# Dealing the rows of a contraction to partitions in fours, and loading one operand by halves of its rows, in a two-layer matmul with GELU

## The chip, the cores and the metric

One core of one Trainium2 chip. The metric is device time in microseconds, the median of several executions. The kernel before takes 124.92 us (three runs, 124.63 to 124.98). Profiles are of one execution each, and their spans are 1.7 to 2.0 us shorter than the device time. In the views PE is TensorE, PEld its weight loads, DVE VectorE, ACT ScalarE and POOL GpSimd.

## The reference

```python
# a 1024x1024, b 1024x2048, c 2048x1024, all float32
h = a @ b
h = 0.5*h*(1 + tanh(sqrt(2/pi)*(h + 0.044715*h**3)))
return h @ c
```

## The kernel before

The first product is made with its rows h transposed: b is the stationary operand, a turned by 90 degrees (`aT`) the moving one. The second is one level of a Strassen scheme over 2x2 blocks. The change concerns the first stage: the first 512 rows of a against the first 768 columns of b, in eight slices of k of 128 each.

```python
av = a.rearrange("(mt p) k -> p mt k", p=128)
bv = b.rearrange("(kt p) n -> p kt n", p=128)      # slice k: 128 rows in succession
# ...
for k, n in ((0, 1), (1, 1), (2, 2), (4, 2), (6, 2)):
    load_a0(k, n)            # n*128 columns of 512 rows: runs of 512 or 1024 bytes
    for i in range(n):
        load_b0(k + i)       # 768 columns of 128 rows: runs of 3 KB
nc.gpsimd.tensor_copy(gate, b_st[5][:, 0:1])       # GpSimd's own loads start when b_5 has landed
# ... ten matmuls on zeros, to warm TensorE up ...
for k in range(KT):
    ab = abf.tile([128, 4, 128], BF16, name="ab")
    nc.vector.tensor_copy(ab, a_st[k])             # cast
    pt = tpool.tile([128, H], BF16, name="pt")
    for j in range(4):
        nc.tensor.transpose(pt[:, ts(j, 128)], ab[:, j, :], ident)
    nc.vector.tensor_copy(aT[0][:, k, :], pt)      # copy out of PSUM
    for i in range(2):
        nc.scalar.activation(b_lo[:, k, ts(i, W0 // 2)], b_st[k][:, ts(i, W0 // 2)], AF.Copy)
    if k > 0:
        mm0(k - 1)                                 # six matmuls 128x512 of the slice before
mm0(KT - 1)
# ... next columns of b (loaded by GpSimd), the other half of a, and so on: PE without a break ...
```

## Time and profile before

| | before |
|---|---|
| median | 124.92 us |
| span of the profiled run | 123.0 us |
| first matmul of the first stage | 7.87 us |
| first matmul of the stage after it | 22.10 us |

The last two are read from the timeline (start, length, engine, line, operation):

```profile
7.87 1.46 PE L102 MATMUL ps<-aT,b_lo 128*128 128x512 bf16 x6
...
22.10 0.60 PE L134 MATMUL pt<-aT,b_lo 128*128 128x512 bf16 x2
```

The page of the profile has a row per engine over the span in 40 equal slices (about 3.1 us each). A digit is the busy share in tenths; PEclk is the granted clock of TensorE; GB/s is what the DMA engines moved. Of the kernel before:

```profile
PE   6955889999998999999999999999999999999990
...
PEclk9999999999999999999999999999999999999997
...
GB/s 108 198 358 384 379 295 193 205 202 203 212 206 206 316 398 238 206 208 103 0 3 0 5 0 0 0 0 55 201 0 0 5 85 113 143 195 146 171 143 113
```

After the seventh slice PE is nearly full to the end, and in this run the clock is granted to the last slice. What can move the time is in the first six slices, where PE waits.

### The profile page before, as it was taken

The page shows a single profiled execution, that of the slowest core. Times are in us where ns is not written, and L with a number is a line of the kernel's source. Part 1 is how long each engine was busy: PE and PEld are TensorE (multiplying, and loading weights), DVE is VectorE, ACT ScalarE, POOL GpSimd, SP SyncE. Part 2 cuts the span into 40 slices and gives each one's busy share as a digit, 9 for nine tenths or more (in the row PEclk, how much of TensorE's full clock was granted, in tenths as well). Part 3 has the DMA queues.
Part 4 walks back from the last instruction along what each step waited for, and adds up shares of the span by engine and source line. Part 5 has one row for each costly group of instructions (what it writes and reads, how often), then busy time and mean ns, then how long its engine had stood idle before and what let it go on. Part 6 is the DMA issues. An engine that isn't in the chain of part 4 may idle for free.

```text
span 123.0 us, 1436 instructions
## 1 busy us (share of the span) xinstructions
PE 114.0 (93%) x555; PEld 66.8 (54%) x562; DVE 65.2 (53%) x94; ACT 29.6 (24%) x54; POOL 21.1 (17%) x26
## 2 busy tenths in 40 slices
PE   6955889999998999999999999999999999999990
PEld 2323444444456444444444444468888888888860
DVE  0233533000015200007999999999669999964440
ACT  4034545806331133233323333000000000000000
POOL 2000099133440210000000000995000000000000
PEclk9999999999999999999999999999999999999997
DMA  3899999999999999996000000001500023353433
GB/s 108 198 358 384 379 295 193 205 202 203 212 206 206 316 398 238 206 208 103 0 3 0 5 0 0 0 0 55 201 0 0 5 85 113 143 195 146 171 143 113
DMA packets 14213, 18.43 MB, mean 150 GB/s; under 512 B 768, under 2 KB 9728, under 8 KB 14208
## 3 DMA queue, kind: packets, MB, share of 16 engines
q0 software_dynamic: 7968, 8.91, 39.4%
q1 hardware_dynamic: 6240, 9.44, 22.0%
q8 instruction: 4, 0.07, 0.2%
q14 instruction: 1, 0.01, 0.0%
HBM read 20.97 MB, written 4.19 MB: 205 GB/s over the span
## 4 chain that ended last, share of the span: by engine, by line
PE 82%; DMA 12%; DVE 1%; SPq 1%; issue 1%; DVEq 0%
PE ps L246 41%; PE ps L143 31%; DMA a_st<-in_a_dram 12%; PE ps L102 3%; PE ps L134 3%; PE pt L134 3%; PE pt L162 1%; DVE aT L163 1%; PE pt L110 1%; DVE ab L107 0%; SPq L82 0%; SPq L76 0%; DVE ot L316 0%; DVEq L107 0%
## 5 line engine op out<-in xcount | busy, mean ns | idle before, releaser
L119 ACT ACTIVATE h<-ps 128x512 fp32r<-128x512 f32 (+1 forms) x30 | 17.3, 602 | 27.5 <-PE ps L143 25.2
L143 PE MATMUL ps<-aT,b_hi 128*128 128x512 bf16 x93 | 21.2, 379 | 0.2
L143 PE MATMUL ps<-aT,b_lo 128*128 128x512 bf16 x79 | 17.4, 379 | 0.1
L143 PEld LDWEIGHTS <-b_hi 128*128 128x128 bf16 x96 | 9.3, 98 | 10.8
L246 PE MATMUL ps<-t,s 128*128 128x512 f32 x64 | 15.1, 393 | 0.0
L246 PE MATMUL ps<-t,h 128*128 128x512 f32 x64 | 14.8, 389 | 0.0
L246 PE MATMUL ps<-c,h 128*128 128x512 bf16 (+1 forms) x71 | 14.1, 355 | 0.1
L246 PEld LDWEIGHTS ps<-t,s 128*128 128x128 f32 x64 | 12.0, 188 | 2.6
L246 PEld LDWEIGHTS ps<-t,h 128*128 128x128 f32 x64 | 12.0, 188 | 2.5
L286 POOL COPY lk<-u 128x512 f32<-128x512 f32 x1 | 7.6, 7579 | 33.5 <-ACT u L279 33.5
L143 PEld LDWEIGHTS <-b_lo 128*128 128x128 bf16 x80 | 7.8, 98 | 9.4
L200 DVE TENSOR_TENSOR t<-c,c 128x1024 fp32r<-128x1024 bf16 x4 | 4.7, 1222 | 15.4 <-DMA c<-in_c_dram 15.1
L163 DVE COPY aT<-pt 128x1024 bf16<-128x1024 bf16 x4 | 2.7, 688 | 18.1 <-PE pt L162 18.0
L102 PE MATMUL ps<-aT,b_lo 128*128 128x512 bf16 x47 | 11.5, 379 | 0.1
L246 PEld LDWEIGHTS <-h 128*128 128x128 bf16 x72 | 7.0, 98 | 7.0 <-issue 0.3
L113 ACT ACTIVATE b_lo<-b_st 128x384 bf16<-128x384 f32 x16 | 7.5, 515 | 10.2 <-DMA b_st<-in_b_dram 10.0
L188 POOL DMA_DIRECT2D c<-in_c_dram x8 | 5.9, 743 | 12.3 <-PE ps L143 6.0
L269 DVE TENSOR_TENSOR ot<-ps,u 128x512 f32<-128x512 f32 x11 | 7.3, 682 | 1.1 <-PE ps L246 1.1
L246 PE MATMUL ps<-c,s 128*128 128x512 f32 x32 | 7.4, 389 | 0.0
L107 DVE CAST ab<-a_st 128x512 bf16<-128x512 f32 x8 | 3.7, 463 | 6.0 <-DMA a_st<-in_a_dram 6.0
L246 PEld LDWEIGHTS ps<-c,s 128*128 128x128 f32 x32 | 6.0, 188 | 1.2
L110 PE MATMUL pt<-ident,ab 128*128 128x128 bf16 x32 | 3.2, 223 | 3.7 <-DVE ab L107 3.7
(37 smaller groups left out, 91.4 us busy)
## 6 DMA issues: line engine op xcount, KB each, us to landing
out_dram<-ot SPq DMA_DIRECT2D x15, 256.0 KB, 2.0
b_st<-in_b_dram SPq DMA_DIRECT2D x8, 384.0 KB, 8.6
c<-in_c_dram POOLq DMA_DIRECT2D x6, 512.0 KB, 14.7
c<-in_c_dram POOLq DMA_DIRECT2D x2, 1024.0 KB, 15.0
a_st<-in_a_dram SPq DMA_DIRECT2D x3, 512.0 KB, 8.9
b_hi<-in_b_dram POOLq DMA_DIRECT2D x4, 384.0 KB, 11.2
b_lo<-in_b_dram POOLq DMA_DIRECT2D x2, 512.0 KB, 7.1
ab<-in_a_dram POOLq DMA_DIRECT2D x4, 256.0 KB, 13.8
```

Source lines behind the costliest of these rows:

```text
L102: nc.tensor.matmul(ps[t], bt(k, t), aT[0][:, k, :], start=(k == 0), stop=(k == KT - 1))
L110: nc.tensor.transpose(pt[:, ts(j, 128)], ab[:, j, :], ident)
L113: nc.scalar.activation(b_lo[:, k, ts(i, W0 // 2)], b_st[k][:, ts(i, W0 // 2)], AF.Copy)
L119: nc.scalar.activation(hq[h][t // NH][:, t % NH, :], p, AF.Gelu_apprx_tanh)
L134: nc.tensor.matmul(ps[t], bt(k + i, N0 + t), aT[0][:, k + i, :], start=(k + i == 0), stop=(k + i == KT - 1))
L143: nc.tensor.matmul(p, bt(k, t), aT[h][:, k, :], start=(k == 0), stop=(k == KT - 1))
L163: nc.vector.tensor_copy(aT[1][:, :, ts(j, 128)], pt)
L188: nc.gpsimd.dma_start(out=dst[:, t:t + 4, :], in_=cv[:, r * NH + t:r * NH + t + 4, ts(q, H)])
L200: nc.vector.tensor_tensor(t1[i], c12[:, ts(i, 2), :], c11[:, ts(i, 2), :], op=SUB)
L246: nc.tensor.matmul(p, lhs(t)[:, ts(j, 128)], rhs(t)[:, q], start=(t == 0), stop=(t == NH - 1))
L269: nc.vector.tensor_tensor(ot, u if swap else p, p if swap else u, op=op)
L286: nc.gpsimd.tensor_copy(last_keep, last)
```

## The change

Its intent: row `4p + r` of each block of 512 rows of b goes to partition p, and accordingly column `4c + r` of a belongs to slice r. Then a may be loaded by halves of its rows, in runs of 2 KB instead of 512 or 1024 bytes, and turned with columns four apart. The order of work changes with it: half a row of a holds four slices of k for 128 of the 512 rows, so four turns stand ahead of the first matmul.

```diff
-    bv = b.rearrange("(kt p) n -> p kt n", p=128)
+    bv = b.rearrange("(g p r) n -> p g r n", p=128, r=4)
...
-    for k, n in ((0, 1), (1, 1), (2, 2), (4, 2), (6, 2)):
-        load_a0(k, n)
-        for i in range(n):
-            load_b0(k + i)
+    for mt in range(4):
+        load_a0(0, mt)                  # 128 rows, 512 columns
+    load_b0(0); load_b0(1)
+    load_a0(1, 0); load_a0(1, 1)
+    load_b0(2)
+    load_a0(1, 2); load_a0(1, 3)
+    for k in range(3, KT):
+        load_b0(k)
...
+    def turn0(g, mt):
+        ab = abf.tile([128, 512], BF16, name="ab")
+        nc.vector.tensor_copy(ab, a_st[g, mt])
+        pt = tpool.tile([128, 4, 128], BF16, name="pt")
+        for r in range(4):
+            nc.tensor.transpose(pt[:, r, :], strided(ab, r), ident)
+        nc.vector.tensor_copy(aT[0][:, ts(g, 4), ts(mt, 128)], pt)
+    def cast_b0(k):                     # left half on DVE, right half on ACT
+        nc.vector.tensor_copy(b_lo[:, k, 0:HW], b_st[k][:, 0:HW])
+        nc.scalar.activation(b_lo[:, k, HW:W0], b_st[k][:, HW:W0], AF.Copy)
+
+    for mt in range(4):
+        turn0(0, mt)
+    cast_b0(0)
+    for k in range(KT):
+        if k + 1 < KT and k not in (1, 2):
+            cast_b0(k + 1)
         for t in range(N0):
             nc.tensor.matmul(ps[t], bt(k, t), aT[0][:, k, :], ...)
+            if k in (1, 2) and t in (2, 5):
+                turn0(1, 2 * (k - 1) + t // 3)
+        if k in (1, 2):
+            cast_b0(k + 1)
...
-    for q in range(2):                  # last product: 256 + 256 columns
+    for q0, w in ((0, 384), (384, 128)):
```

Four Strassen sums of 1024 columns become eight of 512 because the staging tiles are now smaller.

More of the change, by code (lines that the diff above doesn't have):

```diff
@@ L40 @@
     keep = ctx.enter_context(tc.tile_pool(name="keep", bufs=1))
-    astage = ctx.enter_context(tc.tile_pool(name="astage", bufs=4))
+    astage = ctx.enter_context(tc.tile_pool(name="astage", bufs=8))
     abf = ctx.enter_context(tc.tile_pool(name="abf", bufs=4))
@@ L72, with load_a0 @@
     a_st, b_st = {}, {}
-    def load_a0(k, n):
-        st = astage.tile([128, 4, 256], F32, name="a_st")
-        nc.sync.dma_start(out=st[:, :, 0:n * 128], in_=av[:, 0:4, ds(k * 128, n * 128)])
-        for i in range(n):
-            a_st[k + i] = st[:, :, ts(i, 128)]
+    def load_a0(g, mt):
+        st = astage.tile([128, 512], F32, name="a_st")
+        nc.sync.dma_start(out=st, in_=av[:, mt, ts(g, 512)])
+        a_st[g, mt] = st
     def load_b0(k):
         st = b0stage.tile([128, W0], F32, name="b0_st")
-        nc.sync.dma_start(out=st, in_=bv[:, k, 0:W0])
+        nc.sync.dma_start(out=st, in_=bv[:, k // 4, k % 4, 0:W0])
         b_st[k] = st
     gate = consts.tile([128, 1], F32, name="gate")
-    for k, n in ((0, 1), (1, 1), (2, 2), (4, 2), (6, 2)):
-        load_a0(k, n)
-        for i in range(n):
-            load_b0(k + i)
+    for mt in range(4):
+        load_a0(0, mt)
+    load_b0(0)
+    load_b0(1)
+    load_a0(1, 0)
+    load_a0(1, 1)
+    load_b0(2)
+    load_a0(1, 2)
+    load_a0(1, 3)
+    for k in range(3, KT):
+        load_b0(k)
     nc.gpsimd.tensor_copy(gate, b_st[5][:, 0:1])
@@ L98, with strided @@
     ps = [ppool.tile([128, H], F32, name="ps") for _ in range(N0)]
-    def mm0(k):
+    def strided(x, r):
+        return x.rearrange("p (c r) -> p r c", r=4)[:, r, :]
+    def turn0(g, mt):
[5 more added lines that the diff above has]
+        nc.vector.tensor_copy(aT[0][:, ts(g, 4), ts(mt, 128)], pt)
+    HW = W0 // 2
+    def cast_b0(k):
[7 more added lines that the diff above has]
+            cast_b0(k + 1)
         for t in range(N0):
@@ L103, in mm0 @@
                              start=(k == 0), stop=(k == KT - 1))
-    for k in range(KT):
-        ab = abf.tile([128, 4, 128], BF16, name="ab")
-        nc.vector.tensor_copy(ab, a_st[k])
-        pt = tpool.tile([128, H], BF16, name="pt")
-        for j in range(4):
-            nc.tensor.transpose(pt[:, ts(j, 128)], ab[:, j, :], ident)
-        nc.vector.tensor_copy(aT[0][:, k, :], pt)
-        for i in range(2):
-            nc.scalar.activation(b_lo[:, k, ts(i, W0 // 2)], b_st[k][:, ts(i, W0 // 2)], AF.Copy)
-        if k > 0:
-            mm0(k - 1)
-    mm0(KT - 1)
+            if k in (1, 2) and t in (2, 5):
+                turn0(1, 2 * (k - 1) + t // 3)
+        if k in (1, 2):
+            cast_b0(k + 1)
     def gelu(t, h, p):
@@ L125, in load_b @@
     def load_b(k0, kn, n0, w):
-        nc.gpsimd.dma_start(out=bcols(k0, kn, n0, w), in_=bv[:, k0:k0 + kn, ds(n0, w)])
+        nc.gpsimd.dma_start(out=bcols(k0, kn, n0, w), in_=bv[:, k0 // 4, k0 % 4:k0 % 4 + kn, ds(n0, w)])
     ps = [(tpool if t < 2 else ppool).tile([128, H], F32, name="pt" if t < 2 else "ps")
@@ L161, in turn @@
         for k in range(KT):
-            nc.tensor.transpose(pt[:, k, :], ab[:, ts(k, 128)], ident)
+            nc.tensor.transpose(pt[:, k, :], strided(ab[:, ts(k // 4, 512)], k % 4), ident)
         nc.vector.tensor_copy(aT[1][:, :, ts(j, 128)], pt)
@@ L193 @@
     load_c(c12, 0, 1)
-    t1 = [astage.tile([128, 2, H], F32R, name="t1", tag="a_st") for _ in range(4)]
+    t1 = [astage.tile([128, 1, H], F32R, name="t1", tag="a_st") for _ in range(8)]
     t2 = [b0stage.tile([128, 1, H], F32R, name="t2", tag="b0_st") for _ in range(8)]
@@ L199, in sum_t1 @@
     def sum_t1(i):
-        nc.vector.tensor_tensor(t1[i], c12[:, ts(i, 2), :], c11[:, ts(i, 2), :], op=SUB)
+        for t in (2 * i, 2 * i + 1):
+            nc.vector.tensor_tensor(t1[t], c12[:, t:t + 1, :], c11[:, t:t + 1, :], op=SUB)
     def sum_t2(t):
-        nc.vector.tensor_tensor(t2[t], c22[:, t:t + 1, :], t1[t // 2][:, t % 2:t % 2 + 1, :], op=SUB)
+        nc.vector.tensor_tensor(t2[t], c22[:, t:t + 1, :], t1[t], op=SUB)
     def sum_s1(t):
@@ L253, in halves @@
         return lambda t: x[t // 4][:, t % 4, :]
-    def pairs(x):
-        return lambda t: x[t // 2][:, t % 2, :]
     def ones(x):
@@ L297 @@
         p = bank()
-        prod(p, whole(s1), pairs(t1), j)
+        prod(p, whole(s1), ones(t1), j)
         combine(4 + j, 1, p, u3[:, j, :])
@@ L310 @@
         combine(4 + j, 0, p, u3[:, j, :], op=SUB, swap=True)
-    for q in range(2):
-        w = H // 2
+    for q0, w in ((0, 384), (384, 128)):
         p = bank(w)
-        prod(p, whole(h12), whole(c21), 3, q=ds(q * w, w))
+        prod(p, whole(h12), whole(c21), 3, q=ds(q0, w))
         ot = new_out()
-        nc.vector.tensor_tensor(ot[:, 0:w], p, last_keep[:, ds(q * w, w)], op=ADD)
-        store(ot, 3, q * w, w)
+        nc.vector.tensor_tensor(ot[:, 0:w], p, last_keep[:, ds(q0, w)], op=ADD)
+        store(ot, 3, q0, w)
 _INS = ['a', 'b', 'c']
```

## The prediction

> **What bounds the kernel now.** I read the chain of waits first, because it says which work set the end. Its opening, in order of time (start, length, what):
>
> ```profile
> 7.21 9.85 DMA a_st<-in_a_dram
> ...
> 17.15 0.53 DVE ab L107
> ...
> 17.73 0.40 PE pt L110 x4
> 18.12 1.29 PE ps L102 x6
> 19.42 0.22 PE pt L110 x4
> 19.64 2.59 PE ps L102 x12
> 22.23 0.48 PE pt L134 x2
> ```
>
> Up to 17.1 us the kernel waits for its first loads (2 MB of a, 3 MB of b). The last piece of a is then cast, turned and multiplied, and the first stage ends at 22.1 us. From there the chain is PE to 119.6 us with 0.7 us of waits, so whatever moves the 22.1 moves the end by as much. Nothing behind it absorbs a delay: the second half's loads, the c loads and the Strassen sums are all tied to the same matmuls.
>
> Next the timeline of the first stage, to see how one slice of a becomes usable:
>
> ```profile
> 5.43 0.46 PE L110 MATMUL pt<-ident,ab 128*128 128x128 bf16 x4
> ...
> 10.15 0.43 DVE L107 CAST ab<-a_st 128x512 bf16<-128x512 f32 x1 [1.66 <-DMA a_st<-in_a_dram]
> 10.63 0.22 PEld L110 LDWEIGHTS <-ab 128*128 128x128 bf16 x4 [1.80 <-DVE ab L107]
> 10.64 0.40 PE L110 MATMUL pt<-ident,ab 128*128 128x128 bf16 x4 [1.31 <-DVE ab L107]
> ...
> 10.87 1.46 PE L102 MATMUL ps<-aT,b_lo 128*128 128x512 bf16 x6
> 11.07 0.42 DVE L111 COPY aT<-pt 128x512 bf16<-128x512 bf16 x1 [0.49 <-PE pt L110]
> ...
> 11.41 0.42 DVE L107 CAST ab<-a_st 128x512 bf16<-128x512 f32 x1
> ```
>
> The reader is to see a round trip: cast on DVE at 10.15, transposes on PE at 10.64, copy out of PSUM on DVE at 11.07, next cast at 11.41. DVE works in program order, cast, copy, cast, copy, so it sits idle 0.49 us while PE turns, and one round trip costs 11.41 - 10.15 = 1.26 us however early the data is there. Before, each round trip readies a whole slice of k, with six matmuls of an earlier slice (1.3 us) beside it, so it is hidden.
>
> Last the view by windows, TensorE only (PE busy, granted clock, DMA share, GB/s):
>
> ```profile
> 5.57:8.98 3.41, 1.66 (x15) 1.00 1.05 347
> 8.98:12.39 3.41, 2.10 (x16) 1.00 1.06 387
> 118.21:121.62 3.41, 1.40 (x13) 1.00 0.47 166
> 121.70:123.00 1.30, 0.00 (x0) 0.50 0.00 0
> ```
>
> I chose windows of 3.41 us. The ten warm-up matmuls, 0.43 us each, end at 5.6, and later ones take 0.216, so full speed begins there. The clock halves near 121.6, after a window with 1.40 us of PE work; 1.66 us at the start kept it.
>
> **What the Trainium skill says.** "TensorE: Matmul & The Clock Gate", Part 1, has a window of 3413 ns that runs freely and halves the clock when PE idled in it; its Part 4 says that transposes do not count as PE-busy the same way. The trace agrees on the window: from 5.57 to 121.62 is 34 of them. The same page, "Weight-path perf modes", allows fast weight load with a column step, so the strided transposes (step 4) should cost what the dense ones do, four in 0.22 us when streaming; no run here shows it yet. "DMA: Bandwidth & Descriptors", "Latency and other measured facts", has a row pitch of 512 KiB at 207 GB/s in each direction and a fall at 2 MiB and up. The 32 KB of this change is far below, so I count nothing for it; before's pitch of b is 8 KB.
>
> **The change, part by part.**
>
> *Loads.* Sixteen DMAs in place of thirteen, same bytes. In the trace's packet records a 512-byte packet takes 27 ns, 1 KB 46, 3 KB 124, and a 2 KB output packet 85. Before: (1024 x 27 + 1536 x 46 + 1024 x 124) / 16 engines = 14.1 us. After: (1024 x 85 + 1024 x 124) / 16 = 13.4 us. So 0.7 us is saved. Landings before fit 2.1 + that sum + 2.9 us of slow start (from b_1 on). With the same losses, after: all of a's first half by 7.1, b_0 8.7, b_1 9.7, a's second half 10.4 to 13.4, b_3 14.4, b_7 18.4.
>
> *What must come before the first matmul.* This is the heart of it. In the new layout a row half of a holds four slices of k, but only 128 of the 512 columns of each. So slice 0 needs all four turns, and the order of instructions on DVE is cast, copy, cast, copy, then the cast of b_0. The first turn waits for the warm-up matmuls, as now: transposes 5.43, copy 5.93 to 6.35. The next casts then start at 6.27, 7.52 and 8.77 (steps of 1.26), the last copy ends near 10.1, and the left half of b_0 (384 columns; estimated 0.36 us from 0.43 for 512) ends near 10.4. First matmul at about 10.45; before it was 7.87. The data is there earlier, so the load does not decide.
>
> *Matmuls with turns among them.* 48 matmuls x 0.216 = 10.4 us. The four turns of the second half stand in k = 1 and 2, every third matmul (0.65 us), against a round trip of 1.26. Step by step: k=0 10.45 to 11.74; turn at 12.39, copy to 13.23, next cast to 13.58; PE, done with its three at 13.26, waits 0.36; that turn's copy ends 14.47, the cast of b_2 behind it 14.75, so PE waits 0.96 ahead of k=2. The same again in k=2: 0.36 and, for b_3, 1.0. So k=3 starts near 17.86, and five slices of 1.294 end at 24.3, against 22.1 before: **+2.2 us**. Every b has landed by then. GpSimd writing descriptors stretched a cast from 0.43 to 0.65 at 18.50; I add 0.2.
>
> *The clock.* From 5.6 to 10.45 PE has only transposes. The window 5.57 to 8.98 would hold about 1.1 us of recorded PE work (the 0.32 that is left of the first turn and two of 0.40), below the 1.40 that ended in half clock. If it drops at 8.98, k=0 runs at 0.43 a matmul until the window ends at 12.39: about +1.0 us, estimated, or about +2.2 if one more window passes. I give a drop 65 in 100, worth 0.8 us on average.
>
> *The rest.* The gate falls with b_5 at 16.4 instead of 15.7, so the next b lands near 21.8, but PE now needs it at 24.3. Eight sums of 128x512 in place of four of 128x1024: about 0.2 us of DVE, behind matmuls. Tail of 384 + 128 columns: the same PE time; the 384-wide add ends later, the store of 64 KB is shorter: -0.1.
>
> Sum: 124.9 + 2.2 + 0.2 + 0.8 - 0.1 = 128.0; with the drop as the likelier case I take 128.2.
>
> **Rivals.**
> 1. *The loads are the bound and PE keeps up.* Then the stage ends at b_7 + cast + six matmuls = 18.4 + 0.5 + 1.3 = 20.2, and PE waits for the next b at about 21.7, so only 0.4 us would be won: 124.5. For it: the chain names DMA for 15 us. Against it: the 1.26 us round trips on DVE, which the chain hides because they overlap today.
> 2. *The slow start of the loads vanishes* (266 GB/s from 3.4 to 8.7 us, 383 after): 122.5 at best if DVE did not bind; it does, so unlikely.
> 3. *No drop of the clock*: 127.2, just within 2%.
> 4. *Strided weight loads are slow*: at twice the 56 ns of a streaming transpose, 32 exposed ones would add some 1.8 us, and the first stage more: 130.
>
> **Range and chances.** No drop gives 127.2, a drop 128.3 to 129.5. 126.5 to 129.9 holds these with half a microsecond on the sides. The line of 2% is at 127.4: with a drop nearly always slower, without one about half. Slower 0.75, within 2% 0.21, faster 0.04.
>
> **What would show it.** In the profile of after: first matmul of L131 near 10.4, with DVE casts (L112) 1.26 us apart ahead of it and "DVE" rather than "DMA" as what PE waited for; idle of about 1 us ahead of k=2 and k=3; stage end at 24 to 26; matmuls of 0.43 us between 9 and 12 if the clock dropped; four strided transposes in 0.22 us. I am wrong if b lands later than I have it, if L131 starts near 8, or if the stage ends at 22 or sooner.

## The result, and the profile after

The changed kernel takes **129.55 us** (four runs, 129.08 to 129.78), against 124.86 us for the kernel before in the same measurement. The ratio is 1.0373, with a 95% interval of 1.034 to 1.041. Ratios here are the mean time of one kernel's fast runs over that of the other's in the same rounds, so they are not quite the ratio of the medians.

The same rows of the page, of the changed kernel:

```profile
PE   6927867999999899999999999999999999999980
...
PEclk9995899999999999999999999999999999999997
...
GB/s 128 255 337 397 408 120 178 193 195 199 209 207 206 319 399 219 207 207 62 0 3 0 0 5 0 0 0 246 0 0 0 5 82 82 155 176 162 164 158 89
```

The loads are indeed ahead: 128 and 255 GB/s in the first two slices in place of 108 and 198. But PE has a 2 in its third slice, and the clock has a 5 in its fourth.

The chain of waits of the changed kernel (start, length, what), which now names no DMA at all in this stretch:

```profile
9.91 0.42 DVE aT L116
10.33 0.28 DVE b_lo L121
...
10.66 3.53 PE ps L131 x9
...
17.89 0.74 DVE ab L112
...
19.13 0.42 DVE aT L116
19.55 0.48 DVE b_lo L121
20.09 6.65 PE ps L131 x30
26.73 0.43 PE pt L154 x2
```

Before the change the matmuls of the next stage began at 22.10; now they begin at 26.57 (the chain books 26.73, when the last matmul ahead of them ends). The 4.5 us between them are nearly all of the 4.7 us by which the spans differ (123.0 and 127.7). The first matmul starts at 10.66 where it was 7.87. Nine matmuls take 3.53 us, counted to the end of the last one; counted in the same way, nine at full clock take 2.12 (run `fill` below). PE waits for the cast of b ahead of k=2 and of k=3:

```profile
16.47 0.82 PE L131 MATMUL ps<-aT,b_lo 128*128 128x512 bf16 x3 [0.79 <-DVE b_lo L121]
...
20.09 6.65 PE L131 MATMUL ps<-aT,b_lo 128*128 128x512 bf16 x30 [0.99 <-DVE b_lo L121]
...
26.57 0.59 PE L154 MATMUL pt<-aT,b_lo 128*128 128x512 bf16 x2
```

The timeline of one of the four turns, up to the cast of the next (in brackets the idle time before an instruction and what ended that):

```profile
7.71 0.42 DVE L112 CAST ab<-a_st 128x512 bf16<-128x512 f32 x1
...
8.19 0.42 PE L115 MATMUL pt<-ident,ab 128*128 128x128 bf16 x4 [0.85 <-DVE ab L112]
8.64 0.42 DVE L116 COPY aT<-pt 128x512 bf16<-128x512 bf16 x1 [0.51 <-PE pt L115]
8.98 0.42 DVE L112 CAST ab<-a_st 128x512 bf16<-128x512 f32 x1
```

From cast to cast is 8.98 - 7.71 = 1.27 us. PE waits 0.85 of it for DVE, and DVE 0.51 for PE; neither waits for a load.

The view by windows of the changed kernel, PE only (PE busy, granted clock, DMA share, GB/s), cut where the clock changed:

```profile
6.74:10.15 3.41, 1.25 (x12) 1.00 1.00 334
10.15:13.56 3.41, 2.90 (x7) 0.50 1.04 411
13.56:16.97 3.41, 2.42 (x17) 1.00 0.94 366
```

One window with 1.25 us of PE work, all of it transposes, is followed by one at half clock, into which the first matmuls fall.

### The profile page after: what moved, and what is told of

It reads as the page before. It is cut to its first block, busy times and chain, and to the rows that moved or that the text cites. A ratio compares the mean times of both kernels' runs of the same rounds, so it can differ in the third digit from the quotient of the medians.

```text
span 127.7 us, 1449 instructions
## 1 busy us (share of the span) xinstructions
PE 116.7 (91%) x562; PEld 67.4 (53%) x562; DVE 68.1 (53%) x106; ACT 26.3 (21%) x46; POOL 17.9 (14%) x26
## 3 DMA queue, kind: packets, MB, share of 16 engines
q1 hardware_dynamic: 4752, 9.44, 20.5%
## 4 chain that ended last, share of the span: by engine, by line
PE 90%; DVE 5%; issue 2%; DVEq 0%
PE ps L267 39%; PE ps L163 30%; PE ps L131 9%; PE pt L103 3%; PE ps L154 3%; PE pt L154 3%; PE pt L115 2%; DVE aT L116 2%; DVE ab L112 2%; PE pt L182 1%; DVE b_lo L121 1%; DVE aT L183 1%; DVEq L359 0%; DVE warm L50 0%; DVE ot L333 0%
## 5 line engine op out<-in xcount | busy, mean ns | idle before, releaser
L163 PE MATMUL ps<-aT,b_lo 128*128 128x512 bf16 x80 | 17.4, 379 | 0.0
L131 PE MATMUL ps<-aT,b_lo 128*128 128x512 bf16 x48 | 12.6, 415 | 2.6 <-DVE b_lo L121 2.6
L267 PE MATMUL ps<-c,h 128*128 128x512 bf16 (+2 forms) x72 | 14.2, 355 | 0.0
L163 PEld LDWEIGHTS <-b_lo 128*128 128x128 bf16 x80 | 7.8, 98 | 9.4
L221 DVE TENSOR_TENSOR t<-c,c 128x512 fp32r<-128x512 bf16 x8 | 5.0, 687 | 12.0 <-DMA c<-in_c_dram 11.9
L131 PEld LDWEIGHTS <-b_lo 128*128 128x128 bf16 x48 | 4.7, 104 | 8.6 <-DVE b_lo L121 3.0
L304 POOL COPY lk<-u 128x512 f32<-128x512 f32 x1 | 4.5, 4502 | 33.4 <-ACT u L297 33.4
L116 DVE COPY aT<-pt 128x512 bf16<-128x512 bf16 x8 | 3.4, 425 | 8.1 <-PE pt L115 8.1
L122 ACT ACTIVATE b_lo<-b_st 128x384 bf16<-128x384 f32 x8 | 4.2, 523 | 13.4 <-DMA b_st<-in_b_dram 13.4
```

The source lines that it names most:

```text
L116: nc.vector.tensor_copy(aT[0][:, ts(g, 4), ts(mt, 128)], pt)
L122: nc.scalar.activation(b_lo[:, k, HW:W0], b_st[k][:, HW:W0], AF.Copy)
L131: nc.tensor.matmul(ps[t], bt(k, t), aT[0][:, k, :], start=(k == 0), stop=(k == KT - 1))
L163: nc.tensor.matmul(p, bt(k, t), aT[h][:, k, :], start=(k == 0), stop=(k == KT - 1))
L221: nc.vector.tensor_tensor(t1[t], c12[:, t:t + 1, :], c11[:, t:t + 1, :], op=SUB)
L267: nc.tensor.matmul(p, lhs(t)[:, ts(j, 128)], rhs(t)[:, q], start=(t == 0), stop=(t == NH - 1))
```

## The experiments

Eleven runs were made. Each stands against the kernel before on the same chip in the same rounds. The chips differ by up to 0.8 us in that kernel's median, so it is the ratios that are compared. All results are correct.

| kernel | median us | before, same rounds | ratio (95%) |
|---|---|---|---|
| changed | 129.55 | 124.86 | 1.0373 (1.034 to 1.041) |
| changed, `again` | 129.70 | 124.88 | 1.0393 (1.034 to 1.044) |
| `fill` | 127.37 | 125.53 | 1.0160 (1.012 to 1.020) |
| `ahead` | 126.66 | 125.53 | 1.0083 (1.001 to 1.016) |
| `bact` | 127.47 | 125.53 | 1.0168 (1.013 to 1.021) |
| `dense` | 129.66 | 125.53 | 1.0342 (1.030 to 1.038) |
| `three` | 125.37 | 124.75 | 1.0043 (0.998 to 1.011) |
| `three_g4` | 125.46 | 124.75 | 1.0036 (0.997 to 1.010) |
| `three_g3` | 125.05 | 124.75 | 1.0012 (0.992 to 1.010) |
| `four_g4` | 125.40 | 124.88 | 1.0019 (0.997 to 1.007) |
| `four_g3` | 125.18 | 124.88 | 1.0016 (0.998 to 1.005) |
| `tail` | 125.00 | 124.75 | 1.0008 (0.997 to 1.005) |

The theory: the loss is (1) four round trips between DVE and PE ahead of the first matmul, (2) the half clock that they bring about, and (3) the casts of b in DVE's queue behind later turns. The rivals: the 32 KB pitch of b's rows, the strided weight loads, or the load as a whole.

### fill: keep the clock

```diff
     for mt in range(4):
         turn0(0, mt)
+        for _ in range(3):
+            nc.tensor.matmul(ps[N0 - 1], warm[:, 0:128], warm, start=True, stop=True)
```

> The changed kernel with three dummy matmuls (128x512, zeros, into a bank that the first real matmul clears) behind each of the first four turns. Theory (clock): PE had too little work from 5.6 to 10.7 us, so the clock was halved for one window and nine matmuls took 3.53 us in place of 1.94. With the dummies the clock stays full: first real matmul still near 10.7, nine of them in 1.9 to 2.0 us, time 1.6 us less than the changed kernel, near 127.9. Rival (slow for another reason, such as waiting for b or for the strided turns): the nine matmuls stay near 3.5 us and the time at 129.5.

127.37 us, ratio 1.0160. The view by windows of `fill`, PE only, has the clock at full where the changed kernel lost it:

```profile
5.87:9.28 3.41, 2.93 (x19) 1.00 0.98 339
9.28:12.69 3.41, 3.13 (x19) 1.00 1.04 402
```

Its timeline has the first nine matmuls in 2.12 us (a group's length includes the whole 0.38 us of the last matmul, though the next could start 0.216 us after it):

```profile
10.62 2.12 PE L133 MATMUL ps<-aT,b_lo 128*128 128x512 bf16 x9
```

The first matmul has not moved (10.62 for 10.66), so twelve matmuls more and the same start make the kernel 2% faster. In the profiles the next stage starts at 24.61 in place of 26.57, 1.96 us earlier. Like for like the clock gave 3.53 - 2.12 = 1.41 us of this, not the 1.6 expected: the 1.94 of the expectation counts nine steps of 0.216 and not the end of the last matmul. Another 0.51 came between the starts of k=2 and k=3 (3.11 us for 3.62): the cast that took 0.73 us in the changed kernel at 17.89 took 0.42 here. By the ratios the gain is larger, 2.1 points or 2.6 us, but these come from two sets of rounds.

That cast runs while GpSimd issues its loads, and in `fill` it does too (at 16.44, the issuing from 16.23 to 17.90), without being stretched. In all profiles the stretched casts of a (0.47 to 0.73 us) lie in GpSimd's issuing, but not every cast that lies in it is stretched. The cause stays open.

### ahead: shorten the round trip

```diff
         for r in range(4):
             nc.tensor.transpose(pt[:, r, :], strided(ab, r), ident)
+        if g == 0 and mt < 3:
+            cast_a0(0, mt + 1)     # the next turn's cast ahead of this turn's copy
         nc.vector.tensor_copy(aT[0][:, ts(g, 4), ts(mt, 128)], pt)
```

> The changed kernel with the casts of a's first half put one turn ahead on DVE (cast 0, cast 1, copy 0, cast 2, copy 1, cast 3, copy 2, copy 3), nothing else. Theory (DVE order): the four round trips of 1.27 us shrink to about 0.85, the first matmul moves from 10.66 to about 9.5, where b_0 (landed 9.03) is the bound, and the time falls by 0.8 to 1.2 us, to about 128.5. Rival (the loads are the bound): the first matmul does not move by more than 0.3 and the time stays at 129.5. The clock may drop all the same.

126.66 us, ratio 1.0083, from the order of three DVE instructions alone. The first matmul moved from 10.66 to 9.07. That is more than expected, because b_0 landed earlier here (it was being cast at 8.33) than in the profiled run of the changed kernel (9.03).

The four runs fall in two groups, and the granted clock tells them apart: 127.38 and 127.49 us at 0.982 and 0.986, 125.93 and 125.81 us at 0.997 and 0.996. The groups differ by 1.6 us. The trace accounts for 1.3 of it: the half-clock window holds 2.68 us of matmuls (second line below), half of which is lost. With two runs in each group, the rest is not told from scatter. With the stretch of idle time now shorter, whether a whole window falls into it depends on the run. The profile is of a run with the drop; by windows, PE only:

```profile
4.93:8.34 3.41, 1.70 (x18) 1.00 0.96 322
8.34:11.75 3.41, 2.68 (x7) 0.50 1.02 380
```

Here 1.70 us of recorded PE work did not keep the clock, while 1.66 us did in the kernel before. The total alone does not decide at this size, and what does stays open. Here the work is 0.42 us of warm-up matmuls and sixteen transposes, there at most eight transposes and 1.1 us of real matmuls. But the last window of the kernel before, with 1.40 us of matmuls alone, was followed by half clock too (third line by windows in the prediction).

### bact: take b's casts out of DVE's queue

```diff
     def cast_b0(k):
-        nc.vector.tensor_copy(b_lo[:, k, 0:HW], b_st[k][:, 0:HW])
-        nc.scalar.activation(b_lo[:, k, HW:W0], b_st[k][:, HW:W0], AF.Copy)
+        for i in range(2):
+            nc.scalar.activation(b_lo[:, k, ts(i, HW)], b_st[k][:, ts(i, HW)], AF.Copy)
```

> The changed kernel with both halves of every b cast on ACT, as before the change, so that DVE has only a's casts and copies. Theory (b's casts sit in DVE's queue behind the turns): the waits of PE for the cast of b ahead of k=2 and k=3 (0.94 and 1.15 us) go, k=3 starts near 17.8 in place of 20.1, the time falls by about 2 us to about 127.3. Rival (these waits hide a wait for b's landing): k=2 and k=3 start no earlier, time at 129.5.

127.47 us, ratio 1.0168. In the timeline of `bact` the waits for b's cast ahead of k=2 and k=3 are gone. What remains are the 0.2 us for a's own cast:

```profile
16.96 0.41 PE L115 MATMUL pt<-ident,ab 128*128 128x128 bf16 x4 [0.20 <-DVE ab L112]
17.21 0.81 PE L131 MATMUL ps<-aT,b_lo 128*128 128x512 bf16 x3
18.22 0.41 PE L115 MATMUL pt<-ident,ab 128*128 128x128 bf16 x4 [0.20 <-DVE ab L112]
18.47 0.38 PE L131 MATMUL ps<-aT,b_lo 128*128 128x512 bf16 x1
```

k=3 starts at 18.47 in place of 20.09. This profiled run had two windows at half clock (8.78 to 15.61), so it hides part of the gain. The next stage starts at 24.95.

### dense: undo the dealing alone

```diff
-    bv = b.rearrange("(g p r) n -> p g r n", p=128, r=4)
+    bv = b.rearrange("(g r p) n -> p g r n", p=128, r=4)
...
-        return x.rearrange("p (c r) -> p r c", r=4)[:, r, :]
+        return x[:, ts(r, 128)]
```

> The changed kernel without the dealing in fours: partition p takes rows p, 128+p, ... of b as before the change (pitch 8 KB in place of 32), and the turns read dense columns. The result stays right, as a is still loaded by halves of its rows. Theory (pitch and strided turns cost next to nothing): time within 0.4 us of 129.5; the weight loads of the turns 98 ns in place of 115, off the path. Rival (the pitch slows the loads or the strided weight loads slow the turns): 1 us or more faster, with b landing earlier or the turns shorter.

129.66 us, ratio 1.0342 (1.030 to 1.038), against the changed kernel's 1.0373 and 1.0393, with which its interval overlaps. The weight loads of the turns take 98 ns here and 111 to 116 with strided columns, yet four transposes take 0.40 us here and 0.41 or 0.42 there. Both rivals fall. The title of the change, the dealing in fours, is a matter of some tenths of a microsecond, if of anything; the order of work that came with it is what costs. The dealing isn't even needed for the 2 KB runs, as this kernel has them too and its result is right.

### three, three_g4, three_g3: all mends together

`three` has the edits of `fill`, `ahead` and `bact` at once. `three_g4` and `three_g3` have the edit of `dense` besides, and the gate of GpSimd's loads on another slice of b:

```diff
-    nc.gpsimd.tensor_copy(gate, b_st[5][:, 0:1])
+    nc.gpsimd.tensor_copy(gate, b_st[4][:, 0:1])     # three_g4; three_g3: b_st[3]
```

> The changed kernel with all three mends at once: dummy matmuls behind the first four turns, a's first casts one ahead, b's casts on ACT alone. Theory (the loss is those three and nothing else, and behind them stands the load): the first stage follows b's landings, its last matmul ends near 20.5, and PE then waits for the next b columns, whose load is held back until b_5 has landed (16.4) and takes 6.2 us, so the next stage starts near 22.5: time 0.2 to 0.8 us above the kernel before, ratio 1.002 to 1.006. Rival (something else in the change costs too, such as the pitch or the sixteen loads): the ratio stays above 1.01.

> As three, without the dealing in fours (contiguous rows of b, dense turns), and the gate of the next b columns on b_4 in place of b_5. Theory: those columns land about 0.9 us earlier, the next stage starts near 21.8, time 0.2 to 0.4 us below the kernel before. Rival (the gate does not bind): as three.

> As three_g4 with the gate on b_3. Theory: the next b columns now share the DMA engines with b_4 to b_7; they land near 20.5, but b_7 lands near 20.5 too and the first stage ends near 22: no better than three_g4, within 0.4 us of the kernel before.

`three`: ratio 1.0043. The three causes, all taken away, give the whole loss back, to within the interval. Singly they took 2.1, 2.9 and 2.0 points off the 3.7% by which the changed kernel is slower, in sum more than the whole. They overlap, and behind them stands another bound. The chain of waits of `three` names it:

```profile
9.19 6.92 DMA b_st<-in_b_dram
...
16.17 0.12 POOL gate L98
16.29 6.12 DMA b_lo<-in_b_dram
22.41 0.05 issue
22.45 0.60 PE pt L166 x2
```

That is the load of b, then the gate, then the load of the next columns of b. PE starts the next stage at 22.45, where it started at 22.10 before.

`three_g4`, 1.0036, and `three_g3`, 1.0012: the gate was what held `three` (in both profiles PE no longer waits for the next columns), but the first stage ends at 21.8 and 22.1 instead, and nothing is won that can be told from the kernel before. The gain of 0.2 to 0.4 us that was expected of `three_g4` did not come.

### four_g4, four_g3: an attempt to beat the kernel before

```diff
-        if g == 0 and mt < 3:
-            cast_a0(0, mt + 1)
+        if mt < 3:
+            cast_a0(g, mt + 1)
...
-        for _ in range(3):
+        for _ in range(2):
```

> three_g4 with two dummies a turn in place of three (three of them, 0.65 us, were on PE's own path once the casts ran ahead) and with the casts of a's second half one ahead as well. Theory (PE's turns still hold the first stage: about 0.6 us of dummies and three waits of 0.7 us for a cast among k=1 and k=2): k=3 starts when b_3 is cast, near 15.1, the first stage ends near 21.5 in place of 22.0, if the next b columns have landed by then; time 0.2 to 0.5 us below the kernel before, ratio 0.996 to 0.999. Rival (the loads hold it in any case): ratio 1.00 to 1.005 as for three.

> four_g4 with the gate on b_3. Theory: the next b columns land before the first stage ends, so they never hold PE; b_4 to b_7 land a little later; ratio 0.995 to 1.000. Rival (sharing the engines delays b_7 by as much as it wins): no better than four_g4.

1.0019 and 1.0016: missed. With PE's own waits taken away, the loads bound the stage: in the profile of `four_g4` the next columns of b land at 22.64 although their gate opened at 15.74, and in that of `four_g3` k=3 waits for b_3 until 15.2, where `three_g4` had it a little sooner. All five mended kernels and the one before start the next stage between 21.8 and 22.7. I found no version that beats the kernel before.

### again: the changed kernel once more

> The changed kernel itself once more, on the chip of these two, to see how the time goes with the phase of the clock's window. Theory: ratio 1.034 to 1.040 as in the first measurement; every run has a granted clock below 0.985, as the idle stretch of about 5 us always covers most of one window; runs with lower clock are longer, by half of the time at half clock less what the waits absorb. Rival (the drop was chance): some runs at 0.995 and above, some 1.5 us shorter.

Ratio 1.0393. Five of six runs have a granted clock of 0.971 to 0.973 and times of 129.35 to 130.44; none was short. The sixth is a miss for the expectation as written: its granted clock is 1.000 and yet it is the longest (130.94). A likely reading is that the clock's record begins with the first release: the warm-up matmuls of 0.43 us are also shown at 1.00. A run whose first release came late would then show nothing. The kept traces fit this: their record of the clock begins at 5.57 us in the kernel before and at 6.74 in the changed kernel, and holds nothing earlier. But no profile of that run was kept, so for it this was only argued.

### tail: the last product alone

```diff
-    for q in range(2):                      # 256 + 256 columns
+    for q0, w in ((0, 384), (384, 128)):    # in the kernel before
```

> The kernel before with the changed tail alone (the last product in 384 + 128 columns in place of 256 + 256). Theory: the same PE time; the last add is 0.29 us in place of 0.42, but it waits for the 384-wide add, and the store is shorter: 0.0 to 0.2 us less. Rival (the extra wait on DVE costs more than the shorter store wins): 0.1 to 0.3 us more.

Ratio 1.0008 (0.997 to 1.005): no difference that five rounds show.

Its profile shows something else. This kernel has the first stage of the kernel before, and here it lost the clock: the window 4.63 to 8.04 held 0.80 us of PE work, the clock stood at half from 8.04 to 11.46, and six matmuls took 2.77 us in place of 1.46.

```profile
8.82 2.77 PE L102 MATMUL ps<-aT,b_lo 128*128 128x512 bf16 x6
```

Yet the next stage starts at 22.53, 0.4 us later than in the profile of the kernel before, and the run took 125.16 us, as the others did. Of the 22 runs of the kernel before in these rounds, 14 have a granted clock of 0.986 or less; in each set of rounds their mean time is at most 0.4 us above that of the rest. Where PE waits for loads anyway, a window at half clock costs little; in the changed kernel it cost 1.4 us.

## Why the prediction was right or wrong

Predicted 128.2 us (126.5 to 129.9) and slower; measured 129.55. The mechanism held. Two terms of the sum were mis-sized, the clock most (1.4 us, put at 0.8), then the stretched cast (0.6, put at 0.2).

- **What bounds it.** As predicted, nothing behind 22.1 us absorbed the delay: the next stage started 4.5 us later and the span grew by 4.7.
- **The round trips.** Predicted 1.26 us each and the first matmul at 10.45; measured 1.27 and 10.66. The 0.2 came from the first turn: its four transposes took 0.63 us where I had copied 0.46 from the kernel before, because in this run the clock was released only at 6.74 (5.57 in the kernel before), as its record in the trace shows.
- **Turns among the matmuls.** I had PE waiting about 1.0 us ahead of k=2 and of k=3; measured 0.79 and 0.99 (weight loads: 0.94 and 1.15). `bact` shows that it was the cast of b behind the turn.
- **The clock: the term most mis-sized.** "I give a drop 65 in 100, worth 0.8 us on average", with "about +1.0 us" for a drop. The drop came in every profiled run of the changed kernel and of its variants without dummy matmuls, and nine matmuls lost 3.53 - 2.12 = 1.4 us to it. I had let the half-clock window begin at 8.98, before the matmuls, so that part of it passed unused. The window's phase differs from run to run; in this run it began at 10.15, and the first 2.9 us of matmuls fell into it. In `again` it lasted two windows (7.56 to 14.39), which was the other case I had named: from the first matmul to k=2 took 6.46 us there and 4.39 in `fill`, 2.1 more, near the 2.2 of the prediction.
- **GpSimd's interference.** Put at 0.2 us; from k=2 to k=3 the changed kernel took 3.62 us where the plan had 3.06, 0.56 more, with one cast of 0.73 us. As `fill` shows, this is not there in each run, and that GpSimd is the cause was not shown.
- **The loads.** Worked out: 0.7 us less packet time. The page's shares say 22.0% of 123.0 us before and 20.5% of 127.7 after, so 27.1 and 26.2 us per engine, 0.9 less. It bought nothing, as the load was off the path. b_7 was landed at 19.2, not 18.4: from 17.0 on the DMA engines are busy to 0.17 and then 0.10, so on average fewer than three of sixteen carried the end of it.
- **Rivals.** The load as the bound and slow strided weight loads were both ruled out for the changed kernel (`bact`, `dense`); four strided transposes among matmuls took the 0.22 us that was predicted (14.03 to 14.25). But the load is the next bound as soon as the mends are in (`three`), which I had put at 0.4 us below the kernel before and which came out level with it.

Sum as found: 2.2 (turns and waits) + 0.2 (first turn) + 1.4 (clock) + 0.6 (stretched cast) = 4.4 of the 4.5 us.

## What to carry to other kernels

A layout that makes loads longer and fewer may gather several serial steps ahead of the first useful instruction; count the round trips between engines there, at their measured length, before counting bytes. Where two engines hand work to and fro through in-order queues, issue the next item's first step ahead of this item's last one. And count TensorE's work in a stretch of transposes: in these runs the clock fell to half after windows of 3.41 us with 0.80 to 1.70 us of work, and twelve dummy matmuls (2.93 us of work) kept it. Whether that costs anything depends on what bounds the stage (`tail`).

## What the Trainium skill lacked or had wrong

- "TensorE: Matmul & The Clock Gate", Part 1, says that an idle window halves the clock, not how little work counts as idle. Windows of 3.41 us with 0.80 (`tail`), 1.25 (changed kernel, no gap above 0.86 us), 1.63 (`again`) and 1.70 us (`ahead`) of recorded work were followed by half clock; windows with 1.66 us (kernel before) and 1.90 us (changed kernel, 16.98 to 20.39) were not. Part 4's remark that transposes do not count as busy in the same way is neither shown nor refuted: the changed kernel's 1.25 us were transposes alone, but 1.40 us of matmuls alone, at the end of the kernel before, did not keep the clock either.
- The same page's "Weight-path perf modes" allows a column step for fast weight loads but has no cost for it: 111 to 116 ns in place of 98, and 0.01 to 0.02 us in four transposes.
- "DMA: Bandwidth & Descriptors" has pitches of 512 KiB and more only: at 32 KB the time was that of 8 KB to within the intervals (1.0373 and 1.0393 against 1.0342 for `dense`).
- No page says that a profile's granted clock counts the time before the first release as full: the warm-up matmuls at 0.43 us stand under a clock of 1.00, though the record itself begins only at 5.57 us (kernel before).
